# Six modulation units at the end of layer 0's experts, and the z weights' low parts on GpSimd, in a two-layer hybrid diffusion backbone

## The chip, the core and the metric

One core of one Trainium2 chip runs the whole program in one launch. The metric is the device time of that core in microseconds (us). The engines are named as the profile names them: PE (TensorE, matmuls), DVE (VectorE), ACT (ScalarE), POOL (GpSimd) and SP (SyncE, which here only issues loads). Each engine works through its own list of instructions in order; an instruction that waits holds up everything behind it on its engine.

## The reference, cut to what matters

Six modulation vectors per layer come from one conditioning vector: `c @ ada_w[l]` (1024 by 6144), for the latent tokens and for the context tokens. A layer is a mixer and then sixteen experts:

```python
mod_l = jnp.split((s_lat @ ada_w[l] + ada_b[l])[:, None, :], 6, axis=-1)
mod_c = jnp.split(s_ctx @ ada_w[l] + ada_b[l], 6, axis=-1)
h_lat = modulate(rmsnorm(x, norm_g[l, 0]), mod_l[0], mod_l[1])
y_lat, y_ctx = ab_mixer(...) if l % 2 == 0 else ssd_mixer(...)
x = x + mod_l[2] * y_lat
f_lat = modulate(rmsnorm(x, norm_g[l, 1]), mod_l[3], mod_l[4])
x = x + mod_l[5] * expert_choice_ffn(f_lat, ...)      # and the same for ctx in layer 0
# ssd_mixer: p = h @ w_in, of which z is the first 2048 columns
y = (yf + yb + dsk * xs).reshape(bsz, t, SSD_INNER) * jax.nn.silu(z.astype(F32))
```

There are 512 latent and 256 context tokens of width 1024. Layer 0's mixer is HGRN2 with neighbourhood attention; layer 1's is a Mamba-2 SSD mixer with 8 groups.

## The kernel before, in words

The program is one straight list of stages: layer 0's mixer, its experts, layer 1's SSD mixer, its experts, the final norm. All weights stream from HBM in pieces of 0.5 to 1 MB, issued by SP in program order into a few pools of slots; a load waits until the slot's last reader is done. The order of instructions on each engine is made by a scheduler from the written code, which may move independent work forward.

**Products in fp32.** A product is made of three matmuls over a high and a low part of both factors. The high part of a weight tile is a cast on ACT (`S.copy`), the low part a subtraction of the cast from the raw tile. For the SSD weights this is `split` (line 702 the cast, line 703 the subtraction, 128 by 1024 elements each); `load_split` loads a raw tile `w_raw` and splits it in two halves. Each SSD group splits three tiles: x, then b with c, then z.

**Modulation units.** `ada_unit` (line 157) makes 256 columns of the modulation: a 1 MB load, 16 matmuls into a 32-row strip, a copy `ada_row` on ACT, one matmul with `sel` that turns it, and the result `modT`. Layer 1 has 24 of them in the list `ada_left`. Before the change eleven of them are worked in the SSD loop (`more_ada`, line 1632: two behind each of the first five groups, one behind the sixth), with their tiles `w_ada` in the same pool as `w_raw`, and four (`NL`) in layer 1's router.

**The end of layer 0's experts.** `moe_both` takes expert by expert, `up(e)` and then `down(e-1)`. The last expert has no `up` behind it, and its `down` takes the split tiles of its second weight matrix from slots of the loader that are free by then (`ld.spare`, eight `spare` casts on ACT at line 513). Each expert's rows `ye` are added to `xd` in HBM by a scatter on POOL; the last expert's (and one more's) are kept in SBUF as `ye_s`. Then the six tiles `x_moe` are loaded back from `xd`, and `land` adds the kept rows by one-hot matmuls and twelve DVE additions (line 424). `normalise` takes six sums of squares on ACT (`junk`, line 781), the reciprocal root `rs_y`, and scales `x_moe`; `modulate_T` transposes it (`tp`, `at`) into `xh` and `xl`, on which the SSD mixer's first products wait.

**POOL in the SSD loop** makes `xw`, the factor `R` (line 1610, 128 by 1024, four per group) and the state `st`.

Of the kernel before, what the change touches and what calls it, by code (L numbers as in the profile page):

```python
# [10 lines left out]
F32 = mybir.dt.float32  # L11
# [4 lines left out]
ALU = mybir.AluOpType  # L16
# [11 lines left out]
NT = NTL + NTC  # L28
EPS = 1e-6
WP = 2  # L30
NEXP = 16
# [11 lines left out]

W1, W2 = ((None, None, None, None, None, None, 2, 0), (0, 0, 0, 4, 4, 4, 4, 4)), 8

NAD, NH, NL = (0, 0, 0, 0, 0, 1, 1, 1), 4, 4
NVEC = -(-(_r + 64) // 128) * 128


# [1 line left out]
def kernel(ctx: ExitStack, tc: tile.TileContext, A: dict, out: bass.AP):  # L51
# [23 lines left out]
    def mm(o, l, r, start, stop, **k):  # L75
        return T.matmul(o, l, r, start=start, stop=stop, skip_group_check=True, **k)  # L76
# [98 lines left out]
            V.tensor_tensor(modT[l][:, u * 2:(u + 1) * 2, :], p,  # L175
                            vec("adab", l * 48 + u * 2, 2).unsqueeze(2).to_broadcast([128, 2, 2]), ALU.add)

    last_mm = [None]
    ada_left = [(1, u) for u in (0, 4, 1, 5, 2, 6, 3, 7, *range(8, 24))]

    def more_ada(n, pool=wpool, bank=tp_bank):
# [235 lines left out]
    def land(x, i, kept, s):  # L417

        for j in range(2):
            p = mm_bank()  # L420
            cs = slice(j * 512, (j + 1) * 512)
            for n, (oh, t) in enumerate(kept):
                mm(p, oh[s, i * 128:(i + 1) * 128], t[s, cs], n == 0, n == len(kept) - 1)
            V.tensor_tensor(x[i][:, cs], x[i][:, cs], p, ALU.add)
        return x[i]

    def moe_both(gate, idx, xd, xnd, ld, mp, mq):
# [72 lines left out]
        def down(e, hT):  # L500
            hh, hl = hT
            y = [at_bank() for _ in range(2)]
            for c in range(4):
                w2 = ld.get()
                for kk in range(2):
                    k = c * 2 + kk
                    if e < NEXP - 1:
                        wh, wl = (mp.tile([128, D], F32R, tag="big", bufs=6, name="w2_s") for _ in range(2))
                    else:
                        ld.fetch(len(ld.left))  # L510
                        wt = ld.spare([128, 2, D], F32R)
                        wh, wl = wt[:, 0, :], wt[:, 1, :]
                    S.copy(wh, w2[:, kk, :])  # L513
                    (G if k % 4 == 3 else V).tensor_tensor(wl, w2[:, kk, :], wh.bitcast(F32), ALU.subtract)  # L514
                    for j in range(2):
                        s = slice(j * 512, (j + 1) * 512)
                        mm(y[j][:96], hh[:, k, :], wh[:, s], k == 0, False)
                        mm(y[j][:96], hh[:, k, :], wl[:, s], False, False)
                        last_mm[0] = mm(y[j][:96], hl[:, k, :], wh[:, s], False, k == KT - 1)
            ye = mp.tile([128, D], F32, tag="ye", bufs=2, name="ye")  # L520
            for j in range(2):
                s = slice(j * 512, (j + 1) * 512)
                V.scalar_tensor_tensor(ye[:96, s], y[j][:96], gate[:96, e:e + 1], m5[:96, s],
                                       op0=ALU.mult, op1=ALU.mult)
            G.indirect_dma_start(out=xd[:, :], out_offset=bass.IndirectOffsetOnAxis(ap=idx[:96, e:e + 1], axis=0),
                                 in_=ye[:96, :], in_offset=None, compute_op=ALU.add)
            return ye

        def keep(e, ye):

            f = mp.tile([128, 1], F32, name="oh_i")
            t = mp.tile([128, TOK], F32, tag="gate", bufs=2, name="oh_t")
            o = mp.tile([128, TOK], F32R, tag="xs", bufs=2, name="oh")
            G.iota(t, pattern=[[1, TOK]], base=0, channel_multiplier=0, allow_small_or_imprecise_dtypes=True)
            V.tensor_copy(f[:96], idx[:96, e:e + 1])
            V.tensor_scalar(o[:96], t[:96], f[:96], None, op0=ALU.is_equal)
            h, lo = (mp.tile([128, D], F32R, tag="xg", bufs=XB, name="ye_s") for _ in range(2))
            S.copy(h[:96], ye[:96])
            V.tensor_tensor(lo[:96], ye[:96], h[:96].bitcast(F32), ALU.subtract)
            kept[:] = [(o, h), (o, lo)]  # L540
# [5 lines left out]
        hT = None  # L546
        for e in range(NEXP):
            if e + 2 < NEXP:
                xg.append(rows_of(e + 2))
            h = up(e, xg.pop(0))  # L550
            if e == 1:

                with tc.issue_after(up_mid[0].ins):
                    down(0, hT)
            elif e:
                down(e - 1, hT)
            hT = turn(h)
        x = []
        for i in range(NT):
            x.append(mp.tile([128, D], F32, tag="big", bufs=6, name="x_moe"))  # L560
            SY.dma_start(out=x[i], in_=xd[i * 128:(i + 1) * 128, :])
        keep(NEXP - 1, down(NEXP - 1, hT))
        return [land(x, i, kept, slice(0, 96)) for i in range(NT)]

    def moe_lat(gate, idx, row, x, r, xnd, ld, mp, gt, after):

# [125 lines left out]

    wsp_cur, xh_cur, xl_cur = [None], [None], [None]

    def split(raw, n):

        w = []
        for q in range(2):
            r = raw[:, q * 4:(q + 1) * 4, :]
            t = wsp_cur[0].tile([128, 2, 4, n], F32R, tag="w", name="w_s")  # L700
            wh, wl = t[:, 0], t[:, 1]
            S.copy(wh, r)
            V.tensor_tensor(wl, r, wh.bitcast(F32), ALU.subtract)  # L703
            w.append((wh, wl))
        return w

    def load_split(src, n=256):
        raw = wpool.tile([128, 8, n], F32, tag="w", name="w_raw")
        SY.dma_start(out=raw, in_=src.rearrange("(k p) f -> p k f", p=128))
        return split(raw, n)  # L710

    def cols(src, c0s):

# [62 lines left out]
    def normalise(tiles, pool):  # L776
        ss = pool.tile([128, 8], F32, name="ss")
        junk = pool.tile([128, D], F32, tag="xg", bufs=XB, name="junk")
        nt = len(tiles)
        for i, x in enumerate(tiles):  # L780
            S.activation(junk, x, AF.Square, accum_out=ss[:, i:i + 1])
        for i0, i1 in ((0, NTL), (NTL, nt)):
            if i1 > i0:
                r = rsqrt(ss[:, i0:i1], i1 - i0, 1.0 / D)
                for i in range(i0, i1):
                    V.tensor_scalar(tiles[i], tiles[i], r[:, i - i0:i - i0 + 1], None, op0=ALU.mult)
# [43 lines left out]
    with ExitStack() as mb, ExitStack() as mx:  # L830
# [519 lines left out]
            for u in late:  # L1350
                ada_unit(*u, eng=S)
        g0, i0 = rt.top()
        x = moe_both(g0, i0, xd, xnd, ld, op, oq)
        mod_ab(1, 0)


    with ExitStack() as mb:
# [5 lines left out]
        xl = xT.tile([128, KT, TOK], F32R, tag="xl", name="xl1")  # L1363
        xh_cur[0], xl_cur[0] = xh, xl
        normalise(x, op)
        modulate_T(x, 1, 0, op, range(8))
        release_right()
        release_right()
# [4 lines left out]
        with ExitStack() as sx:  # L1373
# [17 lines left out]
            eb = sp.tile([128, 64, 4], F32, name="eb")  # L1391
            sp = sx.enter_context(tc.tile_pool(name="ssd", bufs=1, side="right"))

            w = load_split(w_in[:, 6144:6208], 64)
            pl, pc = gemm_fm(w, 0, m=64)
            dt = sp.tile([64, TOK], F32, tag="xw", name="dt")
            e_ = sp.tile([64, TOK], F32, tag="mt", bufs=2, name="dte")
# [98 lines left out]
            for g in range(8):  # L1496
# [3 lines left out]
                zs = sp.tile([128, 2, LAT], F32, tag="zs", name="zs")  # L1500
                xk = sp.tile([128, NT, 256], F32, name="xk", bufs=2)
                bk = sp.tile([128, NT, 128], F32, name="bk")
                w = load_split(w_in[:, 2048 + g * 256:2048 + (g + 1) * 256])
                for m in range(2):
                    pl, pc = gemm_fm(w, m * 128)
                    conv(pl, pc, g * 2 + m, xg[:, m, :], nu)
# [54 lines left out]
                for n in range(3):  # L1561
# [11 lines left out]
                    else:  # L1573
                        for d in range(2):
                            V.tensor_tensor(st[:, n + 1, d], st[:, n + 1, d], pc[n - 1 if d == 0 else 2 - n][:, d], ALU.add)
                w = load_split(w_in[:, g * 256:(g + 1) * 256])
                for m in range(2):
                    pl, _ = gemm_fm(w, m * 128, ctxp=False)

# [246 lines left out]
```

## Time and profile before

| | |
|---|---|
| time, median of 3 runs | 2381.79 us (2377.67 to 2385.51) |
| the profiled execution's own time | 2383.91 us |
| its span, first to last instruction | 2382.2 us |
| mean granted clock of TensorE | 0.976 of full |
| busy in the span | PE 94%, DVE 53%, ACT 35%, POOL 21% |
| SSD mixer's groups, start to start | 64.5 to 71.5 us |

The profile and the trace are of one execution. Starts are in us from the span's start. In a row of the timeline the bracket at the end gives the idle time of the engine ahead of the instruction and what ended it. "x4" says how many like instructions the row holds; its duration is that of all of them.

### The profile page before, as it was taken

To read this page: it belongs to the slowest core of one execution; us is meant where nothing else is said; L and a number is where in the kernel's file an instruction comes from. 1 tells how busy PE (TensorE), PEld (TensorE's weight loads), DVE (VectorE), ACT (ScalarE), POOL (GpSimd) and SP (SyncE) were. 2 spreads that over 40 slices of the span, in tenths; PEclk is the share of its full clock that TensorE was granted. 3 is DMA by queue.
4 is the path that set the end of the run, shared out by engine and by line. 5 is a ranking of instruction groups with operands and counts; after the bars stand their busy time and mean duration, and the time that the engine had idled before them with its cause. 6 is when DMAs were issued, how large, how long until landed. Compare 5 with 4: busy or idle time off the path is not lost.

```text
span 2382.2 us, 37593 instructions
## 1 busy us (share of the span) xinstructions
PE 2233.0 (94%) x15522; PEld 1395.8 (59%) x15522; DVE 1272.6 (53%) x2237; ACT 845.3 (35%) x1396; POOL 508.0 (21%) x383
## 2 busy tenths in 40 slices
PE   7999999899999999999988999999999999988886
PEld 6888887877344444444466778777777733322222
DVE  5566476635343433443587888877885512222224
ACT  4446454522242443343453444443443211111111
POOL 1000044421121322221322433334442000000001
PEclk9999999999899999999988999999999999999999
DMA  8554311239999999999533333333256999999996
GB/s 270 162 162 151 102 37 46 80 125 347 345 368 365 370 379 387 367 393 346 174 102 111 104 109 116 124 117 106 72 197 222 377 364 418 419 419 418 419 418 263
DMA packets 253707, 587.94 MB, mean 247 GB/s; under 512 B 14240, under 2 KB 129056, under 8 KB 253536
## 3 DMA queue, kind: packets, MB, share of 16 engines
q1 hardware_dynamic: 240960, 548.44, 61.0%
q0 software_dynamic: 5280, 18.88, 3.1%
q10 hardware_dynamic: 7296, 18.22, 2.2%
q8 instruction: 122, 2.00, 0.3%
q14 instruction: 49, 0.40, 0.1%
HBM read 560.99 MB, written 24.51 MB: 246 GB/s over the span
## 4 chain that ended last, share of the span: by engine, by line
PE 21%; DVE 13%; DMA 12%; ACT 2%; issue 1%; POOL 1%; SPq 0%; ACTq 0%; DVEq 0%; POOLq 0%
PE mm L76 11%; DMA w_moe<-in_w_dram 8%; PE at L76 5%; DVE acc L1471 4%; DVE mt L1605 2%; PE tp L76 2%; PE o L76 1%; DVE w_s L703 1%; DMA R<-acd 1%; DMA w_raw<-in_ssd_w_in_dram 1%; DVE mt L1608 1%; DMA yin<-yd 1%; PE tp L87 0%; DVE bT L1476 0%; DVE xg L1476 0%
## 5 line engine op out<-in xcount | busy, mean ns | idle before, releaser
L76 PE MATMUL mm<-w_moe,xs 128*32 128x512 f32 (+1 forms) x4080 | 597.9, 598 | 19.4 <-DMA w_moe<-in_w_dram 19.3
L76 PE MATMUL mm<-xh,w_s 128*128 128x512 f32 (+2 forms) x1824 | 475.1, 357 | 5.1 <-ACT z L1068 3.7
L76 PEld LDWEIGHTS mm<-w_moe,xs 128*32 128x32 f32 (+1 forms) x4080 | 171.7, 117 | 397.5 <-issue 336.4
L76 PEld LDWEIGHTS mm<-xh,w_s 128*128 128x128 f32 (+1 forms) x1824 | 306.3, 189 | 55.0 <-issue 5.9
L76 PE MATMUL mm<-xl,w_s 128*128 128x512 f32 (+1 forms) x912 | 293.7, 356 | 0.0
L76 PEld LDWEIGHTS mm<-xl,w_s 128*128 128x128 f32 x912 | 159.2, 189 | 24.5 <-issue 3.5
L76 PE MATMUL at<-w_s,hT_h 128*96 128x512 f32 x480 | 162.8, 405 | 1.6 <-POOL w_s L514 1.1
L514 DVE TENSOR_TENSOR w_s<-w_moe,w_s 128x1024 fp32r<-128x1024 f32 x90 | 126.9, 1432 | 62.8 <-ACT w_s L513 59.9
L1471 DVE SCALAR_TENSOR_TENSOR acc<-u,cwh,acc 128x770 f32<-128x770 f32 (+1 forms) x128 | 145.0, 1146 | 10.1 <-ACT acc L1468 8.7
L514 POOL TENSOR_TENSOR w_s<-w_moe,w_s 128x1024 fp32r<-128x1024 f32 x30 | 75.0, 2499 | 334.4 <-ACT w_s L513 274.2
L513 ACT CAST w_s<-w_moe 128x1024 fp32r<-128x1024 f32 x120 | 124.4, 1049 | 46.6 <-PE at L76 22.0
L76 PE MATMUL at<-w_moe,o 128*64 128x512 f32 x512 | 120.1, 600 | 9.6 <-DMA w_moe<-in_w_dram 8.0
L478 DVE TENSOR_TENSOR ha<-mm,ha 128x512 f32<-128x512 f32 x16 | 11.1, 691 | 217.9 <-PE mm L76 217.2
L1610 POOL TENSOR_TENSOR R<-R,cT 128x1024 f32<-128x1024 f32 x32 | 99.5, 3124 | 127.8 <-ACT R L1609 71.1
L76 PEld LDWEIGHTS at<-w_s,hT_h 128*96 128x96 f32 x480 | 75.1, 161 | 59.3 <-issue 22.6
L477 ACT ACTIVATE ha<-mm 128x512 f32<-128x512 f32 x16 | 9.6, 597 | 260.5 <-PE mm L76 260.5
L753 DVE TENSOR_TENSOR w_s<-w_raw,w_s 128x1024 fp32r<-128x1024 f32 x56 | 74.1, 1328 | 46.3 <-ACT w_s L752 46.2
L76 PE MATMUL at<-w_s,hT_l 128*96 128x512 f32 x240 | 94.2, 393 | 0.0
L628 DVE TENSOR_TENSOR ha<-mm,ha 128x512 f32<-128x512 f32 x16 | 11.1, 691 | 147.6 <-PE mm L76 147.6
L76 PE MATMUL mm<-w_s,xh 128*128 128x256 f32 x480 | 89.5, 291 | 0.2
L657 DVE SCALAR_TENSOR_TENSOR m<-at,gateS,m 64x512 f32<-64x512 f32 x32 | 24.0, 750 | 121.5 <-PE at L76 113.3
L627 ACT ACTIVATE ha<-mm 128x512 f32<-128x512 f32 x16 | 9.6, 597 | 223.5 <-PE mm L76 223.5
(463 smaller groups left out, 3729.7 us busy)
## 6 DMA issues: line engine op xcount, KB each, us to landing
w_moe<-in_w_dram SPq DMA_DIRECT2D x380, 1024.0 KB
w_ada<-in_ada_w_dram SPq DMA_DIRECT2D x40, 1024.0 KB
w_raw<-in_ssd_w_in_dram SPq DMA_DIRECT2D x16, 1024.0 KB
R<-acd ACTq DMA_DIRECT2D x32, 512.0 KB
w_raw<-in_ab_w_in_dram SPq DMA_DIRECT2D x12, 1024.0 KB
spare<-in_ada_w_dram SPq DMA_DIRECT2D x8, 1024.0 KB
w_raw<-in_ssd_w_in_dram SPq DMA_DIRECT2D x16, 512.0 KB
w_raw<-in_ssd_w_out_dram SPq DMA_DIRECT2D x8, 1024.0 KB
```

Source lines behind the costliest of these rows:

```text
L76: return T.matmul(o, l, r, start=start, stop=stop, skip_group_check=True, **k)
L478: V.tensor_tensor(ha, B[1], ha, ALU.mult)
L513: S.copy(wh, w2[:, kk, :])
L514: (G if k % 4 == 3 else V).tensor_tensor(wl, w2[:, kk, :], wh.bitcast(F32), ALU.subtract)
L628: V.tensor_tensor(ha, B[1], ha, ALU.mult)
L657: V.scalar_tensor_tensor(t[p, s], y[q, :], gate[q, e:e + 1], m5[q, s], op0=ALU.mult, op1=ALU.mult)
L703: V.tensor_tensor(wl, r, wh.bitcast(F32), ALU.subtract)
L753: V.tensor_tensor(wl, r, wh.bitcast(F32), ALU.subtract)
L1471: V.scalar_tensor_tensor(acc[:, :n], u[:, i:i + n], cwh[:, i * 32 + cblk:i * 32 + cblk + 1], acc[:, :n], op0=ALU.mult, op1=ALU.add)
L1605: V.tensor_scalar(mt[:, hh, c, :], R[:, hh, c, :], acT[:, c, h:h + 1], adT[:, c, h:h + 1], op0=ALU.min, op1=ALU.subtract)
L1608: V.tensor_tensor(mt, mt, cb[d].unsqueeze(1).to_broadcast([128, 2, 4, 128]), ALU.mult)
L1610: G.tensor_tensor(R, R, cT.rearrange("p (a b) -> p a b", a=4).unsqueeze(1).to_broadcast([128, 2, 4, 128]), ALU.mult)
```

## The change

`moe_both` fetches what is left of the experts' weights after the last `up` and then issues six loads of modulation weights (`load_ada(NE)`, NE = 6) into slots of the loader that have come free. The six units are worked after the last `down`: two ahead of the landing, one each behind the landing of tiles 1 and 3, two behind it, all with their result on ACT. Five units stay in the SSD loop (two, two and one). The first SSD loads, of the time steps (`dt`) and of group 0's x columns, are issued only behind the last `x_moe` load. The last scatter is written further down. The z weights' low parts are subtracted on POOL (`eng=G`), sixteen halves in all.

```diff
-NAD, NH, NL = (0, 0, 0, 0, 0, 1, 1, 1), 4, 4
+NAD, NH, NE, NL = (0, 0, 0, 0, 0, 1, 1, 1), 4, 6, 4
@@ down(), the last expert's split tiles
                     else:
-                        ld.fetch(len(ld.left))
                         wt = ld.spare([128, 2, D], F32R)
@@ the loop over experts
             h = up(e, xg.pop(0))
+            if e == NEXP - 1:
+                ld.fetch(len(ld.left))
+                late = ld.load_ada(NE)
@@ the end of moe_both
-            SY.dma_start(out=x[i], in_=xd[i * 128:(i + 1) * 128, :])
-        keep(NEXP - 1, down(NEXP - 1, hT))
-        return [land(x, i, kept, slice(0, 96)) for i in range(NT)]
+            x_last[0] = SY.dma_start(out=x[i], in_=xd[i * 128:(i + 1) * 128, :])
+        ye = down(NEXP - 1, hT)
+        keep(NEXP - 1, ye)
+        def ada(n, mm_):
+            with tc.issue_after(mm_.ins):
+                for _ in range(min(n, len(late))):
+                    ada_unit(*late.pop(0), eng=S)
+        ada(2, last_mm[0])
+        for i in range(NT):
+            land(x, i, kept, slice(0, 96))
+            ada(int(i in (1, 3)), land_mm[0])
+        ada(len(late), land_mm[0])
+        return x, lambda: scatter(NEXP - 1, ye)
@@ split and load_split
-            V.tensor_tensor(wl, r, wh.bitcast(F32), ALU.subtract)
+            eng.tensor_tensor(wl, r, wh.bitcast(F32), ALU.subtract)
@@ layer 1
         normalise(x, op)
+        last_scatter()
...
-            w = load_split(w_in[:, 6144:6208], 64)
+            with tc.issue_after(x_last[0].ins):
+                w = load_split(w_in[:, 6144:6208], 64)
...
-                w = load_split(w_in[:, 2048 + g * 256:2048 + (g + 1) * 256])
+                with tc.issue_after(x_last[0].ins):
+                    w = load_split(w_in[:, 2048 + g * 256:2048 + (g + 1) * 256])
...
-                w = load_split(w_in[:, g * 256:(g + 1) * 256])
+                w = load_split(w_in[:, g * 256:(g + 1) * 256], eng=G)
```

On SP, at the seam between layer 0's experts and the SSD mixer, this stood before (the first two `w_raw` are dt's and the x columns', the pair is b and c):

```order
L395 DMA w_moe<-in_w_dram 128x2x1024 x184
L709 DMA w_raw<-in_ssd_w_in_dram 128x8x64
L709 DMA w_raw<-in_ssd_w_in_dram 128x8x256
L1514 DMA w_raw<-in_ssd_w_in_dram 128x8x128 x2
L561 DMA x_moe<-xd 128x1024 x6
L709 DMA w_raw<-in_ssd_w_in_dram 128x8x256
L162 DMA w_ada<-in_ada_w_dram 128x8x256 x2
```

And on SP at the same place now:

```order
L396 DMA w_moe<-in_w_dram 128x2x1024 x184
L404 DMA spare<-in_ada_w_dram 128x8x256 x6
L568 DMA x_moe<-xd 128x1024 x6
L728 DMA w_raw<-in_ssd_w_in_dram 128x8x64
L728 DMA w_raw<-in_ssd_w_in_dram 128x8x256
L1536 DMA w_raw<-in_ssd_w_in_dram 128x8x128 x2
L728 DMA w_raw<-in_ssd_w_in_dram 128x8x256
L163 DMA w_ada<-in_ada_w_dram 128x8x256 x2
```

The six modulation loads stand ahead of everything, and `x_moe` has moved ahead of the mixer's first four loads.

On ACT, from the last expert's eight casts to the first `xh` of layer 1, this stood before:

```order
L513 CAST spare<-w_moe 128x1024 x8
L702 CAST w_s<-w_raw 128x256 x2
L702 CAST w_s<-w_raw 128x1024
L538 CAST ye_s<-ye 96x1024
L781 ACTIVATE junk,ss<-x_moe 128x1024 x6
L771 ACTIVATE xh_10639<-tp,modT_100,A_10625 128x512 x2
```

And on ACT now, from the fourth square to the first `xh` (three units' copies and the dt casts stand ahead of this piece):

```order
L800 ACTIVATE junk,ss<-x_moe 128x1024
L169 COPY ada_row<-tp 128x128
L800 ACTIVATE junk,ss<-x_moe 128x1024
L174 ACTIVATE modT_100<-tp,vecT 128x2 x2
L721 CAST w_s<-w_raw 128x1024
L169 COPY ada_row<-tp 128x128
L800 ACTIVATE junk,ss<-x_moe 128x1024
L174 ACTIVATE modT_100<-tp,vecT 128x2 x2
L169 COPY ada_row<-tp 128x128
L174 ACTIVATE modT_100<-tp,vecT 128x2 x2
L790 ACTIVATE xh_10788<-tp,modT_100,A_10774 128x512 x2
```

The cast of the first x columns (`w_s<-w_raw 128x1024`), once ahead of the squares, now stands between the fifth and the sixth, and the first `xh` stands behind it and behind all six units.

On POOL, in the SSD loop over two groups, this stood before:

```order
L1550 TENSOR_TENSOR xw<-xk,weT 128x256 x10
L1610 TENSOR_TENSOR R<-R,cT 128x1024 x2
L1563 TENSOR_TENSOR st<-st,eb 128x256 x6
L1610 TENSOR_TENSOR R<-R,cT 128x1024 x2
L138 TENSOR_TENSOR rs_y<-rs_t,negh 128x4
L1550 TENSOR_TENSOR xw<-xk,weT 128x256 x10
```

And on POOL now, at the third and fourth group:

```order
L1572 TENSOR_TENSOR xw<-xk,weT 128x256 x10
L1632 TENSOR_TENSOR R<-R,cT 128x1024 x2
L1585 TENSOR_TENSOR st<-st,eb 128x256 x6
L1632 TENSOR_TENSOR R<-R,cT 128x1024 x2
L722 TENSOR_TENSOR w_s<-w_raw,w_s 128x1024
L139 TENSOR_TENSOR rs_y<-rs_t,negh 128x4
L722 TENSOR_TENSOR w_s<-w_raw,w_s 128x1024
L1572 TENSOR_TENSOR xw<-xk,weT 128x256 x10
```

The two z halves stand behind the group's last `R`, with `rs_y` of the group between them.

## Rows read from the trace of the kernel before

**Rows 1.** The page's first part: busy time and share of each engine.

```profile
PE 2233.0 (94%) x15522; PEld 1395.8 (59%) x15522; DVE 1272.6 (53%) x2237; ACT 845.3 (35%) x1396; POOL 508.0 (21%) x383
```

**Rows 2.** Windows, group to group of the SSD loop: length, busy time, clock, DMA share, GB/s.

```profile
1554.30:1625.80 71.50, 69.13 (x487) 55.22 (x487) 58.66 (x90) 31.56 (x48) 26.53 (x21) 0.98 0.34 111
...
1690.30:1758.20 67.90, 62.76 (x400) 49.12 (x400) 57.39 (x86) 28.94 (x44) 29.02 (x21) 0.97 0.28 90
sum 472.70, PE 453.37 PEld 362.60 DVE 391.34 ACT 203.54 POOL 190.79; mean PE 64.77 PEld 51.80 DVE 55.91 ACT 29.08 POOL 27.26
```

**Rows 3.** The chain that ended last, 1285 to 1500: start, us, what.

```profile
1431.16 4.83 DMA w_raw<-in_ssd_w_in_dram
...
1460.55 1.14 DVE w_s L703
...
1499.03 6.04 DMA w_raw<-in_ssd_w_in_dram
```

**Rows 4.** The same chain, 1500 to 1700.

```profile
1567.42 4.81 DMA w_raw<-in_ssd_w_in_dram
...
1606.20 5.25 DMA w_raw<-in_ssd_w_in_dram
```

**Rows 5.** Windows of the SSD loop, the matmuls on `w_ada` alone (PE, PEld).

```profile
1352.60:1419.70 67.10, 2.96 (x64) 1.89 (x64) 1.00 0.35 118
...
1690.30:1758.20 67.90, 0.00 (x0) 0.00 (x0) 0.97 0.28 90
```

**Rows 6.** The same window, `ada_row` alone (PE, PEld, ACT).

```profile
1352.60:1419.70 67.10, 0.66 (x4) 0.67 (x4) 0.54 (x2) 1.00 0.35 118
```

**Rows 7.** One line, L514 in layer 0's experts, by shape: count, ns min/median/max.

```profile
L514 DVE TENSOR_TENSOR w_s<-w_moe,w_s x90: 1207/1215/2823, 631.0 to 1170.3; 128x1024 fp32r<-128x1024 f32 x90
...
L514 POOL TENSOR_TENSOR w_s<-w_moe,w_s x30: 2370/2395/3427, 666.2 to 1171.7; 128x1024 fp32r<-128x1024 f32 x30
```

**Rows 8.** The page's costliest groups: the same subtraction on DVE, busy and mean.

```profile
L514 DVE TENSOR_TENSOR w_s<-w_moe,w_s 128x1024 fp32r<-128x1024 f32 x90 | 126.9, 1432 | 62.8 <-ACT w_s L513 59.9
```

**Rows 9.** One line, L703 in the SSD loop: count, ns min/median/max.

```profile
L703 DVE TENSOR_TENSOR w_s<-w_raw,w_s x42: 1208/1224/3458, 1292.4 to 1743.2; 128x1024 fp32r<-128x1024 f32 x42
```

**Rows 10.** Timeline of DVE from 1690: start, us, engine, line, operation.

```profile
1690.47 3.46 DVE L703 TENSOR_TENSOR w_s<-w_raw,w_s 128x1024 fp32r<-128x1024 f32 x1 [0.24 <-ACT w_s L702]
```

**Rows 11.** Timeline of POOL, 1470 and 1690.

```profile
1470.20 1.01 POOL L138 TENSOR_TENSOR rs_y<-rs_t,negh 128x4 f32<-128x4 f32 x1 [18.68 <-DVE rs_t L137]
...
1690.46 5.68 POOL L1610 TENSOR_TENSOR R<-R,cT 128x1024 f32<-128x1024 f32 x2 [2.17 <-DVE cT L1476]
```

**Rows 12.** Windows at the end of layer 0's experts (columns as in Rows 2).

```profile
1160.00:1170.00 10.00, 9.29 (x48) 5.17 (x41) 9.07 (x10) 7.48 (x11) 2.60 (x1) 1.00 0.00 0
1170.00:1180.00 10.00, 7.99 (x34) 5.04 (x34) 8.95 (x8) 8.85 (x10) 6.84 (x3) 1.00 0.00 1
...
1190.00:1200.00 10.00, 6.24 (x16) 4.27 (x17) 6.71 (x9) 4.34 (x7) 0.00 (x0) 0.69 1.03 390
```

**Rows 13.** Timeline of SP there.

```profile
1181.53 1.79 SPq L709 DMA_DIRECT2D w_raw<-in_ssd_w_in_dram  x2
...
1188.47 3.64 SPq L561 DMA_DIRECT2D x_moe<-xd  x6
```

**Rows 14.** Timeline of PE there: landing matmuls, then the first transposes.

```profile
1191.69 0.96 PE L76 MATMUL mm<-ye_s,oh 96*128 96x512 f32 x3 [3.24 <-ACT ye_s L538]
...
1195.86 6.75 PE L76 MATMUL mm<-ye_s,oh 96*128 96x512 f32 x18 [1.58 <-DVE x_moe L424]
1206.65 2.58 PE L87 MATMUL tp<-ident,x_moe 128*128 128x128 f32 x8 [4.04 <-DVE x_moe L786]
```

**Rows 15.** Timeline of DVE and of ACT there.

```profile
1195.12 2.69 DVE L424 TENSOR_TENSOR x_moe<-x_moe,mm 128x512 f32<-128x512 f32 x4 [2.04 <-DMA x_moe<-xd]
...
1203.94 1.06 ACT L781 ACTIVATE junk<-x_moe 128x1024 f32<-128x1024 f32 x1 [0.29 <-ACT junk L781]
1209.06 1.45 ACT L771 ACTIVATE xh<-tp,modT,A 128x512 fp32r<-128x512 f32 x2 [3.97 <-PE tp L87]
```

More of the change, by code (lines that the diff above doesn't have):

```diff
@@ L176, in ada_unit @@
                             vec("adab", l * 48 + u * 2, 2).unsqueeze(2).to_broadcast([128, 2, 2]), ALU.add)
-    last_mm = [None]
+    last_mm, land_mm, x_last = [None], [None], [None]
     ada_left = [(1, u) for u in (0, 4, 1, 5, 2, 6, 3, 7, *range(8, 24))]
@@ L422, in land @@
             for n, (oh, t) in enumerate(kept):
-                mm(p, oh[s, i * 128:(i + 1) * 128], t[s, cs], n == 0, n == len(kept) - 1)
+                land_mm[0] = mm(p, oh[s, i * 128:(i + 1) * 128], t[s, cs], n == 0, n == len(kept) - 1)
             V.tensor_tensor(x[i][:, cs], x[i][:, cs], p, ALU.add)
@@ L524, in down, with scatter @@
                                        op0=ALU.mult, op1=ALU.mult)
+            if e < NEXP - 1:
+                scatter(e, ye)
+            return ye
+        def scatter(e, ye):
             G.indirect_dma_start(out=xd[:, :], out_offset=bass.IndirectOffsetOnAxis(ap=idx[:96, e:e + 1], axis=0),
                                  in_=ye[:96, :], in_offset=None, compute_op=ALU.add)
-            return ye
         def keep(e, ye):
@@ L693, with split @@
     wsp_cur, xh_cur, xl_cur = [None], [None], [None]
-    def split(raw, n):
+    def split(raw, n, eng=V):
         w = []
@@ L702, in split, with load_split @@
             S.copy(wh, r)
-            V.tensor_tensor(wl, r, wh.bitcast(F32), ALU.subtract)
+            eng.tensor_tensor(wl, r, wh.bitcast(F32), ALU.subtract)
             w.append((wh, wl))
         return w
-    def load_split(src, n=256):
+    def load_split(src, n=256, eng=V):
         raw = wpool.tile([128, 8, n], F32, tag="w", name="w_raw")
         SY.dma_start(out=raw, in_=src.rearrange("(k p) f -> p k f", p=128))
-        return split(raw, n)
+        return split(raw, n, eng)
     def cols(src, c0s):
@@ L1352 @@
         g0, i0 = rt.top()
-        x = moe_both(g0, i0, xd, xnd, ld, op, oq)
+        x, last_scatter = moe_both(g0, i0, xd, xnd, ld, op, oq)
         mod_ab(1, 0)
```

## The prediction

> **What bounds the kernel now.** I read the page's busy shares first. PE is busy 94% of the span and every other engine about half or less [rows 1], so by the average it is PE's work that counts. An average over stages does not say which wait ends last in the two stages that the change touches, so I went to windows by stage.
>
> The SSD loop, group to group, lasts 472.7 us over seven intervals, with PE busy 453.4 and DVE 391.3 [rows 2]. PE looks like the limit with 4% to spare, but the chain of waits says that the limit changes hands: in the first part of an interval it runs through PE and through loads of `w_raw` of 4.8 to 6.0 us [rows 3, 4], in the second through DVE, where even the subtractions of the splits stand on the chain [rows 3]. The reader is to see two things in rows 2. The interval with two units at 1554 lasts 71.5 with PE busy 69.1; the one at 1690, without any unit, lasts 67.9 with PE busy only 62.8. Taking PE work away shortens an interval as long as DVE does not take over.
>
> The end of layer 0's experts is the other stage. From 1160 to 1180 the DMA share is 0.00, and from 1190 to 1200 PE is busy 6.24 of 10 us at a granted clock of 0.69 [rows 12]. PE sits idle there 3.24 us ahead of the landing, 1.58 in it and 4.04 ahead of the transposes [rows 14]: 8.9 us in which other matmuls would cost nothing.
>
> **The change part by part.**
>
> *Units out of the loop.* Two units take 2.96 us of PE for their `w_ada` matmuls [rows 5] and 0.66 for the turn [rows 6], so one is worth 1.81 us and six 10.9. Lower bound 0: the units fill waits for DVE. Upper bound: the slots that they give back let the `w_raw` loads go early, and the three waits of 6.04, 4.81 and 5.25 us [rows 3, 4] go as well, 16.1 more, 27.0 in all. I take 10.9: PE is the fuller engine in each interval, and the interval without a unit still lasts 67.9 [rows 2], so more than PE's own time is not borne out. What is late next in the second half of a group is DVE.
>
> *z's low parts on POOL.* Sixteen subtractions of 1.22 us leave DVE [rows 9], at most 19.5 us if all stand on the chain, as the one at 1460 does [rows 3]. On POOL the same shape takes 2.40 [rows 7], and POOL is idle 18.7 us ahead of `rs_y` in a group [rows 11], so POOL has the room. The price is what DVE loses beside it. In layer 0's experts DVE's mean is 1.432 [rows 8] against a median of 1.215 [rows 7]: 90 times 0.217 spread over 30 POOL operations is 0.65 us for each. In the loop a DVE subtraction that began beside `R` on POOL took 3.46 instead of 1.22 [rows 10, 11], 2.24 lost to one operation. So a half moved is worth between 1.22 − 0.65 = 0.57 gained and 2.24 − 1.22 = 1.02 lost, and the sixteen between −9.1 and +16.3; if POOL cost DVE nothing, −19.5. I take 0: the halves stand where POOL was idle, nearer to the cheaper row, but behind them wait `rs_y` of the group and the z matmuls, which get the low part 1.2 us later. That makes the loss up to the gain.
>
> The row at 1690 shows a DVE instruction that lasts almost as long as POOL's beside it. The Trainium skill (page "SBUF — State Buffer", section "Who interferes with whom") has it that the port pair which the two engines share is an exclusive lock, that a DVE instruction with two SBUF inputs contends with a GpSimd one that reads SBUF, and that the later one is fully blocked. This trace agrees in that row (3.46 against 1.22) and not in the mean of layer 0's experts (1.432). By that rule, with every half met by a two-input DVE instruction, the term would be the upper end above, by the rows +16.3.
>
> *The end of layer 0's experts.* The six loads go into a stretch in which DMA is idle [rows 12], so they cost nothing; if they landed late, the units would wait in front of the landing. The units' PE time, 10.9 us, meets 8.9 us of idle PE [rows 14], and the landing matmuls are paced by DVE's additions, so it fits almost. `x_moe` is loaded ahead of the mixer's tiles instead of behind them [rows 13]; DVE's wait of 2.04 for it [rows 15] goes, and what is late next is `ye_s`. I count 1.2 gained there. Against it: the dt load now waits for the third unit's slot and the x columns' load for the same slot behind dt's subtraction. The third unit is worked after the second landed tile, which was done at 1195.12 + 2.69 = 1197.8 [rows 15] and comes 1.2 earlier, about 1196.6; dt, a quarter of 1 MB, lands some 4 us later, an estimate below the 4.81 of the larger tiles [rows 4], about 1201; its split takes about 1.5, an estimate from the 1.22 of a larger half [rows 9], and the x columns, 1 MB, take 5.25 more [rows 4], to about 1207.7. Their cast stands on ACT ahead of the sixth square, as the order shows. So the sixth square, which began at 1203.94 [rows 15], begins about 1208.6 and ends about 1210, and the first `xh`, at 1209.06 before [rows 15], comes after it and after two results of units, about 1212.5. The loss is 3.5 us, and the 1.2 of the landing is lost in it. Bounds: −1 (the slot comes free earlier, and only the landing's gain is left), and +7 (PE at the clock of 0.69 needs 10.9 / 0.69 = 15.8 us for the units, 6.9 more than the idle time). I take +3.5. The eighth of the spare casts waits for PE to have used the fourth before it; PE has two more parts in hand then, so I cost it within that.
>
> *The last scatter* keeps its place on POOL and costs nothing: it waited for an engine that is idle.
>
> **The sum.** −10.9 + 0 + 3.5 = −7.4 on the execution's own 2383.9, 2376.5. The median of the runs is 2.1 below that execution, so the forecast is 2374. Layer 1's experts begin when the mixer ends, and the chain runs through from one to the other, so a saving in the loop moves the end by as much.
>
> **The rivals.**
>
> A, slower: POOL blocks DVE. The place is the second half of each group, where DVE sets the pace; the price is 1.02 us for each half [rows 9 to 11], and since DVE then sets the pace throughout, the units give nothing. All sixteen: +16.3 + 3.5 = +19.8, 2401.6; half of them: +8.2 + 3.5 = +11.7, 2393.5. It decides for "slower" (7.1 us) from four halves up, (7.1 − 3.5) / 1.02, if the units give nothing. For it: the row at 1690, and that the interval without units is no shorter. Against it: PE is busy 62 to 69 us of every interval, and POOL is idle where the halves go.
>
> B, units in PE's holes: PE waited anyway, and the units are worth 0 to 4. Then −2 + 0 + 3.5 = +1.5, 2383. For it: 67.9 us without a unit [rows 2]. Against it: that interval holds the blocked subtraction of 3.46, and the one with the most PE work is the longest.
>
> C, the waits for `w_raw` go too: −10.9 − 16.1 + 3.5 = −23.5, 2358; with half of them 2366. For it: three waits on the chain stand where a unit's tile held the slot. Against it: in the interval without units no such wait is on the chain, and it is not shorter.
>
> That the change doesn't do what it says is ruled out by the order: six modulation loads stand ahead of `x_moe`, and the z halves stand on POOL.
>
> **How the numbers follow.** A measurement of this kernel can tell 0.3%, 7.1 us, from no change: faster is under 2374.6, slower over 2388.9. The forecast has 0.46, with a range of its own from 2366 to 2383; it lies on the border, so 0.26 of that is faster and 0.20 the same. C has 0.20, all faster. B has 0.15, 0.13 of it the same and 0.02 slower. A has 0.19, slower; 0.02 of the chance of the same I give to slower, for the upper bound at the seam. Together: faster 0.46, same 0.31, slower 0.23. The range takes in C to its full size and A to the half: 2358 to 2394.
>
> **What would show it.** Right: the intervals that lose units shorten by 2 to 4 us; DVE's subtractions and convolutions keep their medians; the modulation loads land before 1181; the first `xh` comes 2 to 5 us later. Wrong: DVE instructions of 2.4 us and more beside the z halves, intervals that last 66 us and more without a unit (A); intervals unchanged with PE's busy time down (B); no `w_raw` on the chain in the loop and intervals under 63 us (C). If the sixth square is not held by the x columns, the term at the seam is wrong.

## The result: 0.5% slower

The changed kernel takes 2395.38 us (median of 7 runs), the kernel before 2382.16 (7 runs); the ratio is 1.0051, 95% interval 1.0033 to 1.0068. The forecast was 2374 in a range of 2358 to 2394. The changed kernel's profiled execution took 2388.40 us, 7.0 below its median, and before's 2383.91, 1.8 above; so the two traces show 4.5 of the 13.2 us. The rest does not show as one place in them: layer 0's mixer, which the change does not touch, ended 5.0 us earlier in the changed kernel's execution, and over all profiled executions below its end lies between 624.9 and 631.4.

Below are the page's busy times of the changed kernel. PE's fell by 8.1, but DVE's rose by 15.4, although sixteen subtractions had left it (answers to [rows 1]).

```profile
PE 2224.9 (93%) x15522; PEld 1392.0 (58%) x15522; DVE 1288.0 (54%) x2215; ACT 847.4 (36%) x1408; POOL 558.5 (23%) x399
```

I divided both spans into stages by marks in the timelines: the first cast of layer 0's experts, the end of their last product, the first `xh` of layer 1, the first `cT` product of group 0 and of group 7, and the first product of layer 1's experts.

| stage, us | before | after | difference |
|---|---|---|---|
| to layer 0's experts | 629.9 | 624.9 | −5.0 |
| layer 0's experts | 558.6 | 558.4 | −0.2 |
| seam, to the first `xh` | 20.6 | 25.0 | +4.4 |
| to group 0 | 76.5 | 70.0 | −6.5 |
| loop, group 0 to group 7 | 472.6 | 485.8 | +13.2 |
| to layer 1's experts | 154.2 | 152.5 | −1.7 |
| layer 1's experts to the end | 469.9 | 470.1 | +0.2 |

The stages ahead of group 0 and behind group 7 move against the loop, since the marks stand in the engines' lists and the scheduler shifts work across them. From the first `xh` to layer 1's experts the difference is +5.0. Each of these spans is of one execution; two executions of one and the same kernel (the extra fills below) differ by 2.8 us in the loop and 2.3 in DVE's busy time there.

These are the windows of the changed kernel's loop, group to group (columns as in [rows 2]):

```profile
1278.20:1347.80 69.60, 62.53 (x432) 49.95 (x429) 57.28 (x83) 28.36 (x42) 32.88 (x23) 0.97 0.34 107
1347.80:1424.20 76.40, 69.79 (x486) 54.67 (x484) 59.79 (x88) 31.54 (x47) 34.99 (x27) 0.98 0.34 110
...
1563.30:1630.00 66.70, 61.63 (x404) 49.05 (x403) 58.19 (x83) 27.43 (x40) 33.19 (x23) 1.00 0.27 87
...
sum 485.80, PE 447.38 PEld 357.48 DVE 412.19 ACT 202.99 POOL 238.37; mean PE 63.91 PEld 51.07 DVE 58.88 ACT 29.00 POOL 34.05
```

DVE is busy 412.2 us where it was 391.3 [rows 2]. Fourteen z halves of 1.22 us fall into these windows and are gone, 17.1 us; so the instructions that stayed last 38.0 us longer in all. The next rows are waits of PE on other engines in that loop (us in total, times, longest), first before, then now: PE's waits for `mt` and for `rs_y` from DVE have grown. Its wait for `cT` has shrunk, from 7.1 to 0.9.

```profile
PE o L76 <- DVE mt L1608: 3.0, 2, 2.6
PE at L1488 <- DVE rs_y L142: 3.0, 2, 2.1
```

```profile
PE o L77 <- DVE mt L1630: 11.1, 4, 4.7
PE at L1509 <- DVE rs_y L143: 7.5, 4, 2.4
```

The seam. The first fence is SP and PE, the second ACT of the changed kernel there (answers to [rows 13 to 15]). The six loads go out at 1145, in 14 us; `x_moe` at 1180; the dt and x loads at 1190.5 over 4.96 us, held by the third unit's slot. The x columns land at 1202.5, and PE waits 5.59 us for the row of a unit whose copy stands behind their cast on ACT.

```profile
1145.08 14.00 SPq L404 DMA_DIRECT2D spare<-in_ada_w_dram  x6
1180.02 2.79 SPq L568 DMA_DIRECT2D x_moe<-xd  x6
1190.50 4.96 SPq L728 DMA_DIRECT2D w_raw<-in_ssd_w_in_dram  x2
...
1197.12 1.08 PE L77 MATMUL tp<-spare,sT 128*32 128x128 f32 x32
1203.79 0.59 PE L77 MATMUL tp<-sel,ada_row 128*128 128x4 f32 x2 [5.59 <-ACT ada_row L169]
```

```profile
1202.53 1.04 ACT L721 CAST w_s<-w_raw 128x1024 fp32r<-128x1024 f32 x1 [3.06 <-DMA w_raw<-in_ssd_w_in_dram]
1203.48 0.26 ACT L169 COPY ada_row<-tp 128x128 f32<-128x128 f32 x1
1203.64 1.06 ACT L800 ACTIVATE junk<-x_moe 128x1024 f32<-128x1024 f32 x1
...
1208.27 0.78 ACT L790 ACTIVATE xh<-tp,modT,A 128x512 fp32r<-128x512 f32 x1 [0.54 <-PE tp L88]
```

### The profile page after: what moved, and what is told of

It reads as the page before. It is cut to its first block, busy times and chain, and to the rows that moved or that the text cites. A ratio compares the mean times of both kernels' runs of the same rounds, so it can differ in the third digit from the quotient of the medians.

```text
span 2386.6 us, 37602 instructions
## 1 busy us (share of the span) xinstructions
PE 2224.9 (93%) x15522; PEld 1392.0 (58%) x15522; DVE 1288.0 (54%) x2215; ACT 847.4 (36%) x1408; POOL 558.5 (23%) x399
## 5 line engine op out<-in xcount | busy, mean ns | idle before, releaser
L77 PE MATMUL mm<-xh,w_s 128*128 128x512 f32 (+2 forms) x1824 | 481.4, 358 | 8.0 <-ACT z L1087 3.7
L1492 DVE SCALAR_TENSOR_TENSOR acc<-u,cwh,acc 128x770 f32<-128x770 f32 (+1 forms) x128 | 159.0, 1247 | 19.0 <-ACT acc L1489 17.3
L514 DVE TENSOR_TENSOR w_s<-w_moe,w_s 128x1024 fp32r<-128x1024 f32 x90 | 126.9, 1431 | 61.6 <-ACT w_s L513 61.2
L514 POOL TENSOR_TENSOR w_s<-w_moe,w_s 128x1024 fp32r<-128x1024 f32 x30 | 74.9, 2498 | 334.2 <-ACT w_s L513 273.9
L478 ACT ACTIVATE ha<-mm 128x512 f32<-128x512 f32 x16 | 9.6, 597 | 260.1 <-PE mm L77 260.1
L1627 DVE TENSOR_SCALAR mt<-R,acT,adT 128x128 f32<-128x128 f32 x256 | 87.5, 414 | 5.1 <-DMA R<-acd 5.0
```

The costliest lines, as they stand in the source:

```text
L1492: V.scalar_tensor_tensor(acc[:, :n], u[:, i:i + n], cwh[:, i * 32 + cblk:i * 32 + cblk + 1], acc[:, :n], op0=ALU.mult, op1=ALU.add)
L1627: V.tensor_scalar(mt[:, hh, c, :], R[:, hh, c, :], acT[:, c, h:h + 1], adT[:, c, h:h + 1], op0=ALU.min, op1=ALU.subtract)
```

## The experiments

Theory 1: the z halves on POOL cost the time, since POOL's operations block DVE; in its form 1a the price is POOL's reading beside DVE, in 1b it is POOL's queue, in which xw, R and `rs_y` come late. Theory 2: the units' move costs it, through the loads that share slots with their tiles.

All times are ratios to the kernel before on the same chip, with 95% intervals; "loop" and DVE's busy time are of the profiled execution, between the same two marks (before: 472.6 and 391.3).

| run | ratio | loop | DVE in it |
|---|---|---|---|
| the change | 1.0051 (1.0033 to 1.0068) | 485.8 | 412.2 |
| units alone | 0.9997 (0.9984 to 1.0011) | 466.2 | 395.3 |
| four units, other slots | 1.0005 (0.9993 to 1.0018) | 465.3 | 393.5 |
| z alone | 1.0048 (1.0029 to 1.0067) | 484.8 | 406.8 |
| change, half of z | 1.0068 (1.0051 to 1.0086) | 495.9 | 413.8 |
| extra reads, half tiles | 1.0051 (1.0033 to 1.0069) | 484.5 | 403.7 |
| extra reads, first half only | 1.0041 (1.0027 to 1.0054) | 483.4 | 404.1 |
| extra reads, whole tiles | 1.0108 (1.0089 to 1.0127) | 493.4 | 419.9 |
| extra fills | 1.0044 (1.0030 to 1.0058) | 475.9 | 395.8 |
| extra fills, again | 1.0026 (1.0015 to 1.0037) | 478.7 | 393.5 |
| column copies alone | 0.9994 (0.9981 to 1.0007) | 473.4 | 389.9 |
| R on DVE | 0.9896 (0.9882 to 0.9911) | 452.3 | 385.1 |
| xw on DVE | 1.0018 (1.0008 to 1.0029) | 474.6 | 403.8 |
| R on DVE, six units | 0.9891 (0.9870 to 0.9912) | 448.6 | 388.3 |
| R on DVE, four units | 0.9886 (0.9867 to 0.9906) | 446.7 | 387.3 |
| the change, R on DVE | 0.9953 (0.9936 to 0.9969) | 467.4 | 400.4 |

### One part at a time

Units alone:

```diff
-                w = load_split(w_in[:, g * 256:(g + 1) * 256], eng=G)
+                w = load_split(w_in[:, g * 256:(g + 1) * 256])
```

> The change with the z weights' low parts back on DVE; the six units stay at the end of layer 0's experts. Theory 1 (the z halves on POOL cost the time: they block DVE and hold up xw and R on POOL; the units are a gain): 2371 to 2380 us, 2 to 11 below before, the SSD loop from first to last group at most 468 us (before 472.6, the change 485.8), the seam from the last product of layer 0's experts to the first xh still about 25 us (before 20.6). Theory 2 (the loss comes from the units' move: the loads of w_raw that share slots with the units' tiles come late, as at 1365 and 1428 in the change): 2390 to 2398 us, the loop 480 us and more.

2380.02 against 2380.29: no difference. The loop came down by 6.4 us, the seam stayed at 25.1. Theory 2 falls; of theory 1 the gain did not come. In that trace the stage ahead of group 0 is also 2.5 us shorter and the one behind group 7 2.6 us longer, so a part of what the loop loses comes back behind it.

z alone, the same line with `eng=G` in the kernel before:

> The kernel before with one change: the z weights' low parts are subtracted on POOL. Theory 1: 2393 to 2406 us (11 to 24 above before), the loop 484 to 496 us, DVE's busy time in the loop higher than before although fourteen subtractions have left it. Theory 2: 2378 to 2386 us, the loop within 4 us of before.

2389.70 us against 2380.29, a little less than theory 1 had forecast; by the intervals the ratio, 1.0048, is that of the change. This is one stretch of that loop, POOL in the first fence and DVE in the second. Four instructions `mt`, which read one tile, last 3.21 us beside the z half, where eight a little later last 2.13; three convolutions, beside the second half and the `xw` right behind it, last 5.49, where three earlier lasted 3.13.

```profile
1460.72 3.07 POOL L703 TENSOR_TENSOR w_s<-w_raw,w_s 128x1024 fp32r<-128x1024 f32 x1 [6.14 <-ACT w_s L702]
...
1475.74 2.40 POOL L703 TENSOR_TENSOR w_s<-w_raw,w_s 128x1024 fp32r<-128x1024 f32 x1 [2.93 <-ACT w_s L702]
```

```profile
1461.44 3.21 DVE L1605 TENSOR_SCALAR mt<-R,acT,adT 128x128 f32<-128x128 f32 x4
...
1465.70 2.13 DVE L1605 TENSOR_SCALAR mt<-R,acT,adT 128x128 f32<-128x128 f32 x8
1467.76 3.13 DVE L1471 SCALAR_TENSOR_TENSOR acc<-u,cwh,acc 128x770 f32<-128x770 f32 x3
...
1474.76 5.49 DVE L1471 SCALAR_TENSOR_TENSOR acc<-u,cwh,acc 128x770 f32<-128x770 f32 x3 [0.35 <-ACT acc L1468]
```

In the whole loop DVE lost 406.8 − 391.3 + 17.1 = 32.6 us to 36.2 us of z halves on POOL, 0.9 us for each us. In this run the scheduler also put DVE's instructions into another order, so it does not yet tell POOL's reading from the order; the runs with extra work below do.

Half of z, in the change: the first half of each tile on DVE, the second on POOL.

```diff
-            eng.tensor_tensor(wl, r, wh.bitcast(F32), ALU.subtract)
+            (eng if q else V).tensor_tensor(wl, r, wh.bitcast(F32), ALU.subtract)
```

> The change with only the second half of each z tile on POOL, the first half on DVE (one POOL operation per group in place of two). Theory 1: halfway between the change and the run with z on DVE, 2382 to 2389 us, the loop 475 to 480 us. Theory 2: as the change, 2392 to 2398 us.

2397.58 us, worse than the whole and in theory 2's range, though the units alone had ruled theory 2 out. So the loss is not in proportion to the number of halves when the scheduler may order all engines anew. The seven halves in its loop are 19.9 us on POOL and DVE lost 413.8 − 391.3 + 8.5 = 31.0; PE waited 10.1 us for `rs_y`, up to 5.1 at a time. Which of the moved instructions made the difference stays open.

Four units, and the two slots that the first SSD loads use left free, z on DVE:

```diff
-                late = ld.load_ada(NE)
+                late = ld.load_ada(2)
+                ld.n += 2
+                late += ld.load_ada(NE - 2)      # NE = 4
```

> z on DVE, and four units instead of six at the end of layer 0's experts, in slots that the first SSD loads do not use; so the loads of dt and of the first x columns no longer wait for a unit. Both theories of the seam: the first xh comes 20 to 22 us after the last product of the experts (25.0 in the change, 20.6 before), the PE wait of 5.6 us there is gone. Theory 1 for the whole: 2370 to 2378 us, 0 to 4 below the run with six units, since two units (3.6 us) go back into the loop and 4.4 us of the seam are saved. Theory 2: 2384 to 2390 us.

The seam is 20.4 us, PE's wait is gone, and the time is that of before (2381.56 against 2380.29), outside theory 1's 2370 to 2378. So the seam's 4.4 us are the wait for the third unit's slot, as both theories had it; the whole did not gain.

### Extra work on POOL, with the other engines' order unchanged

These leave the kernel's work as before and add to POOL, for each z half, something that nobody uses.

```diff
             V.tensor_tensor(wl, r, wh.bitcast(F32), ALU.subtract)
+            if extra:        # z alone
+                G.tensor_tensor(scr[0][:, :2], r[:, :2], wh[:, :2].bitcast(F32), ALU.subtract)
```

> The kernel before, z's low parts on DVE as there, and beside them an extra subtraction on POOL for each z half that reads the same two tiles (half of them, 128 by 512) into a scratch that nobody reads: 16 more POOL operations of about 1.2 us. On DVE, PE, ACT and SP the order of instructions is that of before, word for word. Theory 1a (a POOL operation that reads SBUF blocks DVE for about its own length; the z halves on POOL lost DVE 32.7 us for 36.2 us of POOL in the loop): DVE's busy time in the loop 391 + 14 to 18, the loop 480 to 488 us, 2390 to 2397 us. Theory 1b (not the reads count but POOL's time: xw, R and rs_y come late behind the new operations): DVE's operations keep their lengths, the loop 474 to 480 us.

> As the run with the extra reads of half tiles, but one whole tile (128 by 1024) for the first z half of each group and none for the second: 8 operations of 2.4 us, the same POOL time in half as many pieces; the order on the other engines is that of before. Theory 1a: DVE loses about as much as there, 14 to 18 us, and the loop is 480 to 488 us; a lock that is held longer costs the same in sum. Theory 1b: the loop 474 to 480.

> As above with whole tiles for both halves: 16 extra POOL operations of 2.4 us, the z low parts still on DVE. The order on the other engines differs from before in a few places from the fifth group on. Theory 1a: DVE's busy time in the loop 391 + 28 to 36, the loop 492 to 504 us, 2402 to 2414 us: more than the change itself, since here DVE keeps its subtractions. Theory 1b: 2386 to 2396 us.

With the half tiles the loop is 11.9 us longer and DVE busy 12.4 more, for 27.2 us of extra POOL; with the first half only 10.8 and 12.8, for 18.0; with whole tiles 20.8 and 28.6, for 42.6. The order of DVE, PE, ACT and SP is the same in the first two, and nothing waits for the scratch; so the loss is POOL's reading beside DVE and not the order, nor a low part that comes late.

The two traces show it instruction by instruction, since DVE's list is that of before. In the whole span of the run with half tiles 38 instructions of DVE ran beside one of the 16 extra reads, and together they last 16.1 us longer than the same ones before; all others together last 2.2 less. With the first half only it is 20 instructions beside 8 reads, 16.8 longer, and the others 1.3 less. Theory 1b falls: PE's wait for `R` is 2.9 and 2.6 us there (before 3.3), for `rs_y` 1.2 in both (before 3.0). DVE's extra time is a little below theory 1a's range in the first two runs and in it with whole tiles. In the first two profiles PE, too, is busy 5.1 and 5.9 us more for the same matmuls, at a granted clock of 0.98 and 0.97 where before has 0.99; what that adds to these two loops was not separated.

Fills in place of reads (a copy of one column, then two fills), and the copies alone:

```diff
+                G.tensor_copy(scr[0][:, 0, :1], wh[:, 0, :1].bitcast(F32))
+                G.memset(scr[0], 0.0)
+                G.memset(scr[0], 1.0)
```

> The kernel before with, for each z half, a copy of one column and two fills of 128 by 1024 on POOL into a scratch that nobody reads: POOL is held for as long or longer (I estimate 1.5 to 2 us for each half from the fills of 0.73 us in the trace), but it writes and hardly reads. On DVE, PE, ACT and SP the order is that of before, word for word. Theory 1a: the loop within 4 us of before (472.6), 2377 to 2385 us, DVE's busy time within 5 us of before. Theory 1b: as the run with the extra reads, or worse.

> The run with the extra fills once more, unchanged: its profiled execution was 7 us faster than its median, so what its trace shows may not be what its other executions did. If the fills cost nothing, a median of 2378 to 2385 us; if they block DVE like the reads, 2387 to 2393 us, and a profiled execution near it has DVE's busy time in the loop 10 us and more above before.

> The run with the extra fills without the fills: only the copy of one column for each z half on POOL (0.87 us each there). Order on DVE, PE, ACT and SP as before, word for word. If the fills cost the time: 2378 to 2384 us. If the copies (which read, if only a column) cost it: 2386 to 2392 us, as with the fills.

The copies cost nothing. The fills cost 0.26 to 0.44%, which theory 1a had not expected, and DVE's busy time did not rise by the 10 us that blocking like that of the reads would have meant, but by 2.2 and 4.5. The second profile shows where: the lines of DVE with two tiles as inputs do not get longer (convolutions 1168 ns, 1171 before; `mt` times `cb` 1759, 1843 before), but the one-input `mt` (L1605 before) lasts 428 ns on the mean, 371 before (409 in the first profile). These are the lines of before and then those of the second profile (count, busy us, mean ns, idle ahead):

```profile
L1471 DVE SCALAR_TENSOR_TENSOR acc<-u,cwh,acc 128x770 f32<-128x770 f32 (+1 forms) x112 | 129.7, 1171 | 8.3 <-ACT acc L1468 7.0
L1605 DVE TENSOR_SCALAR mt<-R,acT,adT 128x128 f32<-128x128 f32 x224 | 66.7, 371 | 6.0 <-DMA R<-acd 6.0
...
L1608 DVE TENSOR_TENSOR mt<-mt,cb 128x1024 f32<-128x1024 f32 x28 | 51.0, 1843 | 1.8 <-ACT mt L1607 1.8
```

```profile
L1478 DVE SCALAR_TENSOR_TENSOR acc<-u,cwh,acc 128x770 f32<-128x770 f32 (+1 forms) x112 | 129.4, 1168 | 9.0 <-ACT acc L1475 7.7
L1612 DVE TENSOR_SCALAR mt<-R,acT,adT 128x128 f32<-128x128 f32 x224 | 74.8, 428 | 6.3 <-DMA R<-acd 6.1
```

DVE's list is that of before here too. In the two profiles 73 and 75 instructions ran beside a copy or a fill; added up one by one they last 10.9 and 11.0 us longer than before, 10.8 and 10.7 of it in 23 `mt`. In the run with the copies alone 38 ran beside one, and they last 0.1 us longer. (Neighbouring `mt` overlap, eight in 2.13 us at a mean of 371 ns, so DVE's busy time shows less than this sum.) POOL's two fills and DVE's eight `mt` beside them, in the second profile; eight of them last 2.13 us there where POOL is quiet:

```profile
1462.21 1.04 POOL L708 MEMSET scr<- 128x1024 bf16 x1
1463.31 0.98 POOL L709 MEMSET scr<- 128x1024 bf16 x1
```

```profile
1460.99 3.38 DVE L1612 TENSOR_SCALAR mt<-R,acT,adT 128x128 f32<-128x128 f32 x8
```

This is what the Trainium skill states (page "SBUF — State Buffer", section "Who interferes with whom"): a DVE instruction with two SBUF inputs contends with a GpSimd instruction that reads SBUF and not with one that only writes, while `copy`, `cast` and `tensor_scalar`, which `mt` is, can enter 2-port modes, in which they can contend with GpSimd too. These runs agree, with 1168 against 1171 and 428 against 371; in which mode `mt` worked, no run shows.

### Taking work from POOL

R on DVE, and xw on DVE, each one letter in the kernel before (`G.tensor_tensor(R, R, ...)` to `V.`, and the same for `xw`):

> The kernel before with the product R (128 by 1024, four for each group) on DVE instead of POOL: the reverse of the change, a POOL operation that reads SBUF is taken from the loop. If POOL's operations block DVE for about their own length (theory 1a), the 28 operations in the seven intervals, 86 us on POOL, cost DVE most of the 45 us by which its longest lines exceed their unblocked length (1171 against 970 ns mean for the convolutions, 1843 against 1226 for mt), and on DVE they cost 28 x 1.22 = 34 us: DVE's busy time in the loop between 380 and 400 (before 391), the loop 462 to 474 us, 2370 to 2383 us. If POOL's operations run beside DVE at no cost to it, DVE's busy time is 391 + 34 = 425 and the loop 490 us and more.

> The kernel before with xw (128 by 256, ten for each group) on DVE instead of POOL. On DVE the 70 operations cost about 0.42 us each, an estimate from the 0.416 of another product of the same shape, 29 us, and take 63 us from POOL. Theory 1a: DVE's busy time in the loop 385 to 405, 2375 to 2390 us. If POOL runs beside DVE at no cost: 420, and 2400 us or more.

R on DVE is 1.04% faster, 2355.0 us, a larger gain than theory 1a's 2370 to 2383. DVE takes on 35.1 us of work and is busy 6.2 us less; the convolutions' mean falls from 1171 to 1030 ns and that of `mt` times `cb` from 1843 to 1292. The rows are DVE's costliest lines in that loop (count, busy us, mean ns, idle ahead):

```profile
L1471 DVE SCALAR_TENSOR_TENSOR acc<-u,cwh,acc 128x770 f32<-128x770 f32 (+1 forms) x112 | 113.4, 1030 | 5.5 <-ACT acc L1468 4.6
...
L1608 DVE TENSOR_TENSOR mt<-mt,cb 128x1024 f32<-128x1024 f32 x28 | 35.7, 1292 | 0.0
L1610 DVE TENSOR_TENSOR R<-R,cT 128x1024 f32<-128x1024 f32 x28 | 35.1, 1273 | 0.2
```

And its loop as a whole: PE is busy 449.5 of 452.3 us, so it sets the pace now. Two things came together here: DVE's other instructions last 41.3 us less in sum, and R itself takes 1.27 us where it took 3.10 on POOL, with PE waiting 3.3 us for it before. The scheduler's order is another, too. How much of the loop's 20.3 us each of them gives is not separated.

```profile
1283.20:1735.54 452.34, 449.45 (x3188) 364.05 (x3189) 385.12 (x639) 207.29 (x309) 108.24 (x119) 0.99 0.37 120
```

xw on DVE does not gain: DVE is busy 12.5 more for 25.1 us of new work. So 62.7 us of `xw` had cost DVE 12.6 us, 0.2 for each us, and 86.4 us of `R` 41.3, 0.5 for each: what POOL costs DVE is not one rate for all of its operations.

### The units and z once more, with R on DVE

These are the units alone, the four units and the change, each with R on DVE as above.

> R on DVE as in the run before (2355.0 us), z on DVE, and the change's six units at the end of layer 0's experts. With R on DVE, PE is busy 449 of the loop's 452 us. If the units gave nothing in the change because DVE set the pace (theory U1), they pay now: PE is freed of 8.1 us in the loop, the seam costs 4.5 as with the units alone: 2349 to 2353 us, the loop 443 to 447 us. If they are worth nothing wherever they stand (theory U2: PE had holes for them): 2357 to 2362 us, by the seam.

> R on DVE, z on DVE, and four units in slots that the first SSD loads don't use. Theory U1: PE freed of 5.4 us, the seam as in before: 2347 to 2351 us, the loop 445 to 449 us. Theory U2: 2353 to 2357 us.

> The whole change, z's low parts on POOL, with R on DVE. If a POOL operation that reads SBUF costs DVE its own length whatever else POOL does (theory 1a), z on POOL is a loss here too: 8 to 16 us above the run with six units, 2357 to 2367 us, DVE's busy time in the loop 8 to 16 us above that run's. If z cost time only because it stood in POOL's queue with R (theory 1b, R and xw late), it costs nothing here: within 4 us of the run with six units, or below it.

With six units 2353.47 (0.9891), with four 2352.55 (0.9886), without 0.9896: the loop is 3.7 and 5.6 us shorter than without units, the stage behind it 1.3 and 3.2 us longer, and the intervals of the three ratios overlap, so the units are worth at most a few us and none is shown. The times fit neither theory well: 2353.47 lies between the two, 2352.55 at the lower end of U2's range. With z on POOL 2369.22, 15.8 above the run with six units and a little above theory 1a's range, and DVE busy 12.1 more with fourteen subtractions fewer. Queueing behind R is therefore not what made z dear. The kernel with R on DVE and four units beats before and the change; whether the four units have a part in that is not shown.

## Why the prediction was wrong

**z on POOL: the step that failed.** The term was set at 0, between −9.1 and +16.3. Alone it cost 0.48%, 11.4 us of 2380 (the two medians lie 9.4 apart), and beside six units with R on DVE 15.8. The bounds held it; the choice between them did not. It rested on POOL being idle where the halves go. POOL was idle, but DVE was not, and what counts is which DVE instructions run meanwhile. Of its two prices the prediction went by the lower. The higher one, 1.02 us lost for each half, came from a row of the loop itself [rows 10], and it was the right one: with z alone DVE lost 32.6 us to fourteen halves, 2.33 each, and was spared 1.22, so 1.11 net. The 0.65 us for each POOL operation [rows 7, 8] came from a stage in which DVE waits a good part of the time [rows 8]; whether that is why the price is lower there was not tried. One more thing was missed: the one-input `mt` instructions, 224 in the loop, are slowed as well, from a mean of 371 to 424 ns with z alone, 12.6 us.

**The signs.** Those named for rival A came: beside 15 of the changed kernel's 16 z halves runs a DVE instruction of 2.4 us or more, and the four intervals without a unit last 66.3 to 67.7 us. One that was named for being right came as well: the convolutions keep their median (1022 ns before, 1021 now), while their mean goes from 1171 to 1289. A median does not see a minority of blocked instructions.

**Rival A is what happened in kind**, and the runs with extra reads show its mechanism. That its half, 2393.5, lies so near to the measured 2395.4 is in part luck. The half stood for eight z halves that slow DVE, but 15 of the 16 did; DVE paid the full price, and the time took only about two thirds of it, 11.4 us against 16.3. The half also held +3.5 for the seam, where units and seam together came to nothing. Its second part, that the units give nothing once DVE sets the pace, agrees with the change beside z alone (1.0051 and 1.0048, loops of 485.8 and 484.8); but the units gave nothing with z on DVE either, so DVE's pace is not shown to be the reason.

**The units: the second term that failed.** As a net of −10.9 and +3.5, −7.4, they came to −0.7, with an interval of −3.8 to +2.6. PE's time in the loop fell by 8.1 us in the run with the units alone, from 453.3 to 445.2, for the 204 matmuls of six units; the loop gave 6.4, and the seam took 4.5. I had counted 10.9 by adding busy times of single tiles, which may count twice where neighbouring matmuls overlap. But single profiles do not settle the size: by the same measure four units free PE of 8.5 us, and with R on DVE four free 9.9 and six 4.8. The four units in other slots shorten the loop by 7.3 us at the seam's old length, and the time is the same (1.0005); why, stays open.

In the sum, −10.9 + 0 + 3.5 = −7.4, z was 11.4 too low and the units with the seam 6.7; −7.4 + 11.4 + 6.7 is +10.7, and the ratio of the change gives +12.1.

**The seam** was right in mechanism, place and size: +3.5 foretold, +4.4 measured. The x columns landed 19.2 us after the last product, as in the forecast (1207.7 there). The first `xh` did wait for them, and with them for the third unit's slot; four units in other slots took it away. Not foretold was that PE itself stands for 5.59 us, behind the row of a unit. `x_moe` came early, as foretold. The modulation loads cost nothing that the traces show.

**The loads of `w_raw`** (rival C) went on being late, but fewer of them: the changed kernel's chain has one of 8.36 us at 1365.8 and one of 5.09 at 1428.3 in the loop, and the rows are of that chain. Before it had four, of 4.83, 6.04, 4.81 and 5.25 us [rows 3, 4]; the prediction's upper bound of 16.1 left out the first. So 13.5 us of such waits stand where 20.9 stood, and the loop is longer all the same.

```profile
1365.79 8.36 DMA w_raw<-in_ssd_w_in_dram
...
1428.25 5.09 DMA w_raw<-in_ssd_w_in_dram
```

What they cost beside the blocked DVE was not tried by itself.

## What to carry to other kernels

A busy share of 21% on GpSimd does not make it a free place for work: in these runs each microsecond of a GpSimd operation with input tiles in SBUF cost VectorE between 0.2 and 0.9 us of busy time. Look for VectorE rows that last twice their median and see what GpSimd ran at that moment; if such pairs are there, a gain may lie in taking an operation from GpSimd to VectorE, the other way round from this change; here it did for `R` and not for `xw`. Read the mean and the longest, not the median. And time freed on the fullest engine is no gain yet: with the units out of the loop PE was busy 8.1 us less there, and the kernel took as long as before.

## What the runs showed that I had not expected

- A product of 128 by 1024, 35.1 us of work in 28 pieces, was put on DVE, and DVE's busy time fell by 6.2 us; the kernel became 1.04% faster.
- Fills on POOL, which read nothing, slowed DVE's one-input instructions (428 against 371 ns) and not its two-input ones (1168 against 1171).
- Half of the z halves on POOL cost more (1.0068) than all of them (1.0051); the cause is open.
